# Four gate projections per GLA head, and the first neighbourhood projections beside the last head's rest

## The chip, the cores and the metric

The kernel runs on one core of a Trainium2 chip. Its engines are TensorE (PE), which multiplies matrices, VectorE (DVE), ScalarE (ACT), GpSimd (POOL) and SyncE (SP), whose queue issues the DMAs. Each engine works through its own list of instructions in order, and waits on semaphores for the others. The metric is the device time of one execution in microseconds (us), lower being better.

## The reference

The reference is a backbone of four layers for latent tokens: 1024 tokens of width 1024 on a grid 64 wide, with 256 context tokens ahead. Even layers mix by differential attention and a short gated convolution, odd layers by 2-D neighbourhood attention and a gated linear attention (GLA) that runs in both directions. The change touches the odd layer. Its mixer, cut to what matters:

```python
ck, cv, dk, dv, dlr, cq, dq, cg, dg = split_cols(h @ w_in, ODD_SIZES)
...
gf, gb = gla_log_gates(dlr, gate_up, gate_bias)
qh, kh, vh = to_bht(dq, GLA_DK) * qscale, to_bht(dk, GLA_DK), to_bht(dv, GLA_DV)
_, of = gla_scan(qh, kh, vh, gf, s_f)
_, ob = gla_scan(flip_t(qh), flip_t(kh), flip_t(vh), flip_t(gb), s_b)
o_gla = gla_out(of + flip_t(ob), gnorm)
o_na = neighbourhood_attention(heads(cq, NA_DIM), heads(ck, NA_DIM), heads(cv, NA_DIM), kc_na, vc_na, rpb)
u = jnp.concatenate([o_na.reshape(bsz, seq, BRANCH_W) * jax.nn.silu(cg), o_gla * jax.nn.silu(dg)], axis=-1)
```

In a chunk of the scan, with b the running sum of the log gates, the reference computes

```python
new = exp(b_end) * state + einsum('bhsd,bhse->bhde', kc * exp(b_end - b), vc)
o_inter = einsum('bhtd,bhde->bhte', qf * exp(b), state)
att = einsum('bhtd,bhsd,bhtsd->bhts', qf, kc, decay)     # decay[t, s] = exp(b[t] - b[s]) for s <= t
o = o_inter + einsum('bhts,bhse->bhte', att, vc)
```

There are 4 GLA heads (keys of 128, values of 256) and 16 neighbourhood heads of 64. cg and dg are the gate projections: sixteen blocks of 128 columns, whose SiLU multiplies the outputs.

## The kernel before, in words

**Projections.** Activations and weights are kept as a high and a low part, and a product is made of three (high by high, low by high, high by low). The activations' parts are hA and hB (two buffers, with an h or l behind). A weight unit is 1024x128: it comes by DMA as wraw, ACT casts it to whi (L242), POOL subtracts for wlo (L243). One step of a unit is 24 products `pj` (L438) over one chunk of tokens, 512 columns or 256. The object `ws` hands out steps in the order in which `units1` yields the units: `ws.run(n)` makes the next n, and between units stand named gates. `ws.open(name)` first finishes what stands ahead of a gate, then passes it.

**The GLA head.** `gla_head` walks two groups of 512 tokens (g = 1, 2), each in seven levels (lev 0 to 6; a level's blocks are L = 2^lev long), in `gla_levels`. At each level ACT makes exponentials KQ (L1151), DVE multiplies them by keys and queries (L1153) and adds to the running sums, which are called R in group 1 and g_u in group 2 (L1162), and PE makes the products gl (L1120). Their blocks are merged into att: below L = 32 by one predicated copy of DVE under a mask (L1132), else by copies of ACT, L rows high (L1136). After the levels `gla_exps` makes KH (exponentials on ACT, L1187 and L1188, product on DVE, L1189), g_qb (its product on POOL, L1193) and QF (L1198). `gla_chunk` takes a chunk of 128 tokens: transposes gktr of KH (L1213), split into gkh and gkl, products gu (L1233), the state Sn with its split Sh and Sl (L1258, L1261, L1262), outputs go (L1245). `gla_rest` follows: the last group's chunks, the backward outputs gob (L1337), norms, the transposes gotr (L1362), the multiplication by the stored gate (gsg, L1363), and the store into uT. It gives way twelve times, and a step is run each time.

**Gates.** A gate unit has two steps. Each ends with a tanh on ACT (L213), a product gt on DVE (L214) and a store to sgT (L983). Twelve of the sixteen gate units are run in the scans, three a head, one step at levels 0, 2 and 4 of each group; the last four stand in the rest of head 3.

**Neighbourhood attention.** `na` has 64 units (i, m, bp): eight pairs of heads i, the head m of the pair, a pair of query blocks bp. A unit makes query parts nqd, scores NS (L1464, L1465), bias and minimum on DVE (np, L1468), exp on ACT (L1470), scaling on POOL (L1472), transposes ntr (L1513) split into pth and ptl, and outputs nav (L1490). The bias nB comes from a mask namask and rows nG by DMA (POOL, L1423). Each pair i needs the projections ck (keys nk, L1378), cv (values, transposes nvtr) and cq: eight steps. `ws.until("cq0")` runs the first pair's ahead of everything, and one step goes with each unit after that.

**Order.** Tile's scheduler sets the order on each engine from priorities (the order of the code, moved by `high_priority`) and from when tiles are free. Tiles live in pools; a pool opened over the space of another waits for what was last done there. The neighbourhood pool stands where the GLA's pools stood, and its first tiles wait for the last stores of these.

Of the kernel before, what the change touches and what calls it, by code (L numbers as in the profile page):

```python
# [98 lines left out]
class Kernel:  # L99
# [20 lines left out]
    def setup(self):  # L120
# [20 lines left out]
        self.colsA = c.tile([P, 96], F32, name="colsA")  # L141
# [655 lines left out]
    def out0(self, conv_es, es):  # L797
# [13 lines left out]
        self.mod_finish(0, "g")  # L811
        self.mod_finish(1, "a")
# [126 lines left out]
    def units1(self):  # L939
# [47 lines left out]
    def layer1(self, post, out_es):  # L987
        nc, ws = self.nc, self.ws
        ws.open("gla")
        with ExitStack() as es:  # L990
# [22 lines left out]
        with ExitStack() as es:  # L1013
            ap = self.ap = self.pool("na", ctx=es)
            self.ps_s = self.pool("ps_s1", bufs=1, space=PSUM, ctx=es)
            self.gate_tile = lambda: ap.tile([P, 640], F32, name="gt", tag="np", bufs=5)[:, 0:512]
            self.na()


    def gla_setup(self):  # L1020
# [26 lines left out]
    def gla_v(self, e, ci, t0, tn, ps):  # L1047
# [4 lines left out]
        t = self.gp1.tile([P, 512], F32, name="gvt", tag="T", bufs=2)  # L1052
# [231 lines left out]
    def gla_head(self, h, rest):  # L1284
# [13 lines left out]
        for g in (1, 2):  # L1298
            for lev, _ in enumerate(self.gla_levels(g, R, outs[g])):
# [341 lines left out]
```

## Time and profile before

| | us |
|---|---|
| median of 3 runs | 3097.12 |
| lowest, highest | 3093.14, 3097.38 |
| the profiled execution | 3095.47 |
| its span in the trace | 3093.7 |
| PE busy in the span | 2942.9 (95%) |
| DVE busy | 1879.2 (61%) |
| ACT busy | 1530.6 (49%) |
| POOL busy | 965.5 (31%) |

The profile is of one execution. Busy is the time in which an engine has an instruction under way; PE's matmuls overlap, so that a busy PE is not PE at its peak. The granted clock of PE has a mean of 0.987 of full speed over the span. Layer 1 begins near 1640 us of the span; the heads of the GLA run to some 2285, the neighbourhood attention to 2930, and the last output projection to the end.

### The profile page before, as it was taken

The numbers are of one execution on the slowest core, as the hardware profiler recorded it, in microseconds if no ns is written. First come the engines' busy times: TensorE is split into PE (matmuls) and PEld (weight loads), VectorE is DVE, ScalarE is ACT, GpSimd is POOL, SyncE is SP. The second block draws the span as 40 slices with busy tenths as digits, with TensorE's granted clock in tenths as the row PEclk, the third lists the DMA queues.
The fourth block names the chain that finished last, engine by engine and source line by source line (L and its number), as shares of the span: only waits on it lengthen the run. The fifth ranks groups of instructions, "written<-read, shape, count | busy, mean of one in ns | idle before, by whom it ended". The sixth has DMA issues, their size and how long they took to land. (4 is left out here: it accounts for less than half of the span.)

```text
span 3093.7 us, 42416 instructions
## 1 busy us (share of the span) xinstructions
PE 2942.9 (95%) x16244; PEld 2452.9 (79%) x16244; DVE 1879.2 (61%) x3149; ACT 1530.6 (49%) x2853; POOL 965.5 (31%) x765
## 2 busy tenths in 40 slices
PE   6999999999999999999999998999999999999898
PEld 4888888888888887888877777778777888887686
DVE  5675757575665757564244767575736666667723
ACT  4553535353544445453344665665635555556522
POOL 3213130313021211205233232322235555556622
PEclk9999999999999999999999999999999999999999
DMA  6111111211110211115342112111131111112323
GB/s 227 35 45 48 49 46 33 65 35 58 35 58 28 65 35 48 45 42 207 111 149 74 45 35 72 50 48 58 55 95 31 47 49 44 43 44 98 118 75 123
DMA packets 236982, 206.46 MB, mean 67 GB/s; under 512 B 43591, under 2 KB 194538, under 8 KB 236778
## 3 DMA queue, kind: packets, MB, share of 16 engines
q1 hardware_dynamic: 236778, 203.74, 21.4%
q8 instruction: 128, 2.10, 0.3%
q14 instruction: 76, 0.62, 0.1%
HBM read 168.04 MB, written 35.67 MB: 66 GB/s over the span
## 5 line engine op out<-in xcount | busy, mean ns | idle before, releaser
L243 POOL TENSOR_TENSOR wlo<-wraw,whi 128x1024 fp32r<-128x1024 f32 x149 | 371.6, 2494 | 1164.5 <-ACT whi L242 1014.9
L438 PE MATMUL pj<-hBh,whi 128*128 128x512 f32 (+1 forms) x1712 | 382.0, 353 | 9.7 <-ACT hBh L354 4.8
L438 PE MATMUL pj<-hBl,whi 128*128 128x512 f32 (+1 forms) x1712 | 370.3, 350 | 0.9 <-DVE hBl L355 0.9
L438 PE MATMUL pj<-hBh,wlo 128*128 128x512 f32 (+1 forms) x1712 | 350.7, 345 | 0.0
L242 ACT CAST whi<-wraw 128x1024 fp32r<-128x1024 f32 x176 | 184.5, 1048 | 308.7 <-PE ops L754 188.3
L438 PEld LDWEIGHTS pj<-hBh,whi 128*128 128x128 f32 x1712 | 275.3, 191 | 45.2 <-ACT hBh L354 5.4
L438 PEld LDWEIGHTS pj<-hBh,wlo 128*128 128x128 f32 x1712 | 278.7, 191 | 37.2
L438 PEld LDWEIGHTS pj<-hBl,whi 128*128 128x128 f32 x1712 | 279.5, 193 | 35.7 <-DVE hBl L355 1.1
L438 PE MATMUL pj<-hAh,whi 128*128 128x512 f32 x968 | 279.5, 409 | 14.6 <-ACT ropex L517 13.0
L438 PE MATMUL pj<-hAh,wlo 128*128 128x512 f32 x968 | 255.3, 398 | 0.0
L438 PE MATMUL pj<-hAl,whi 128*128 128x512 f32 x968 | 254.6, 394 | 0.0
L592 DVE TENSOR_REDUCE st<-S 128x1 f32<-128x1280 f32 (+1 forms) x160 | 203.8, 1274 | 79.3 <-PE S L590 79.3
L594 ACT ACTIVATE p<-S,st 128x1280 f32<-128x1280 f32 (+1 forms) x160 | 186.1, 1163 | 82.1 <-DVE st L592 80.5
L1472 POOL TENSOR_TENSOR np<-np,nst 128x640 f32<-128x640 f32 x128 | 166.6, 1304 | 192.3 <-DVE nst L1471 154.4
L438 PEld LDWEIGHTS pj<-hAh,wlo 128*128 128x128 f32 x968 | 181.0, 189 | 36.1
L438 PEld LDWEIGHTS pj<-hAh,whi 128*128 128x128 f32 x968 | 170.2, 191 | 47.9 <-ACT ropex L517 14.4
L438 PEld LDWEIGHTS pj<-hAl,whi 128*128 128x128 f32 x968 | 178.1, 189 | 34.7
L590 PE MATMUL S<-kst,qd 128*128 128x512 f32 (+1 forms) x832 | 192.3, 361 | 0.2 <-ACT p L594 0.2
L590 PEld LDWEIGHTS S<-kst,qd 128*128 128x128 f32 x832 | 137.1, 188 | 40.2 <-ACT p L594 21.5
L1468 DVE CUSTOM_DVE_ANT_0 np<-NS,nB 128x640 f32<-128x640 f32 x128 | 105.3, 823 | 90.4 <-PE NS L1465 84.5
L615 ACT CAST ath<-atr 128x512 fp32r<-128x512 f32 (+1 forms) x208 | 99.2, 505 | 113.5 <-PE atr L612 112.9
L1523 DVE TENSOR_TENSOR ptl<-ntr,pth 128x512 fp32r<-128x512 f32 (+2 forms) x224 | 117.5, 536 | 49.6 <-ACT pth L1522 45.7
(361 smaller groups left out, 6219.3 us busy)
## 6 DMA issues: line engine op xcount, KB each, us to landing
wraw<-in_ev_w_in_dram SPq DMA_DIRECT2D x64, 512.0 KB, 4.1
wraw<-in_od_w_in_dram SPq DMA_DIRECT2D x56, 512.0 KB, 3.9
wraw<-in_w_out_dram SPq DMA_DIRECT2D x55, 512.0 KB, 3.8
wraw<-in_w_mod_dram SPq DMA_DIRECT2D x48, 512.0 KB, 3.8
sgT<-gt SPq DMA_DIRECT2D x32, 256.0 KB, 2.0
uT<-sg SPq DMA_DIRECT2D x8, 640.0 KB, 3.5
nG<-in_rpbp_dram SPq DMA_DIRECT2D x128, 40.0 KB, 2.3
xt<-in_x_dram SPq DMA_DIRECT2D x8, 512.0 KB, 5.9
```

Source lines behind the costliest of these rows:

```text
L242: nc.scalar.copy(out=hi, in_=u.raw)
L243: (nc.vector if u.lo_eng == "v" else nc.gpsimd).tensor_tensor(out=lo, in0=u.raw, in1=hi.bitcast(F32), op=ALU.subtract)
L438: nc.tensor.matmul(ps[:, 0:tn], lhsT=a[:, k, :], rhs=self.h_at(k, t0, tn)[b], start=n == 0, stop=n == 23)
L590: nc.tensor.matmul(S[:, c0:c0 + tn], lhsT=qd[:, 2 * m + part, P * qt:P * qt + P], rhs=self.kst[m][:, t0:t0 + tn], start=part == 0, stop=pa ...
L592: nc.vector.tensor_reduce(out=st[:, m:m + 1], in_=S[:, 0:n], axis=AX.X, op=ALU.max, negate=True)
L594: nc.scalar.activation(out=p[m][:, 0:n], in_=S[:, 0:n], func=AF.Exp, bias=st[:, m:m + 1], accum_out=st[:, 2 + m:3 + m])
L615: nc.scalar.copy(out=dh, in_=tv)
L1468: nc.vector.tensor_tensor_reduce(out=p, in0=S[:, z0:z0 + 640], in1=bias[2 * i + m][:, c0:c0 + 640], scale=1.0, scalar=3e38, op0=ALU.add, o ...
L1472: nc.gpsimd.tensor_tensor(out=p, in0=p, in1=st[:, 2:3].broadcast_to([P, 640]), op=ALU.mult)
L1523: nc.vector.tensor_tensor(out=lv[:, s:e], in0=tr[:, s:e], in1=hv[:, s:e].bitcast(F32), op=ALU.subtract)
```

## The change

The gate units are handed out 4, 4, 4 and 3 to the heads' scans, in another order, and a step is run at levels 0, 2, 4 and 6 of each group. One gate unit is left for head 3's rest. A gate "na1" lets the first neighbourhood projections follow it: in head 3's rest, after its four chunks, `early_na` closes the pools gla1 and gla3 (a new pool that holds Gst, R, att, dec, KH, ql, qh, gkh and gkl) and opens the pool na1 in their space, for nk, nkh, nq, nv, nvt and nvx. The gate "na" stands behind cq0 now, `ws.until("cq0")` is gone, and two steps follow the first scores, not one. The mask lmask has a sixth level, so L = 32 is merged by DVE too. The ring of two tiles T (gt, gvt, graw, QF, gsq, gsg) moves from gla1 to gla2, on the other side of the memory; lrx takes the tag KQ; colsA goes to the rope pool; nvx has its own tile; and the calls of mod_finish are gathered at the end of layer 0's attention. Hunks that only replace one pool by another are left out below.

```diff
--- before.py
+++ after.py
...
@@ -361,6 +360,7 @@
         self.new_h("A")
         self.new_h("B")
         cs = self.pool("rope", ctx=es0)
+        self.colsA = cs.tile([P, 96], F32, name="colsA")
         self.onesD = cs.tile([P, P], F32, name="onesD")
         nc.vector.memset(self.onesD, 1.0 / D)
         self.cos = cs.tile([P, SEQ], F32, name="cos")
@@ -506,6 +506,8 @@
             for h in range(8):
                 self.diff_head(h)
                 self.ws.open(f"head{h + 1}")
+        for l, what in ((0, "g"), (1, "a"), (1, "g")):
+            self.mod_finish(l, what)
         rope_es.close()
         return conv_es
 
...
@@ -952,8 +952,8 @@
             u.hold = u.extra = n == "dq0"
             yield u
         yield "gla0"
-        gates = [8, 9, 0, 1, 10, 11, 2, 12, 13, 3, 14, 15]
-        per = [3, 3, 3, 3]
+        gates = [8, 9, 0, 1, 10, 11, 2, 3, 12, 13, 4, 5, 14, 15, 6, 7]
+        per = [4, 4, 4, 3]
         for h in range(4):
             if h:
                 yield self.proj(f"dk{h}", self.w1(self.DK, h), CHUNKS, lambda *a: self.gla_k(*a))
@@ -964,15 +964,14 @@
             for k in gates[sum(per[:h]):sum(per[:h + 1])]:
                 yield self.gate_unit(k)
             yield f"end{h}"
-        yield self.gate_unit(4)
-        yield self.gate_unit(5)
-        yield self.gate_unit(6)
         yield self.gate_unit(7)
-        yield "na"
+        yield "na1"
         for i in range(8):
             yield self.proj(f"ck{i}", self.w1(self.CK, i), CHUNKS, lambda *a, i=i: self.na_k(i, *a))
             yield self.proj(f"cv{i}", self.w1(self.CV, i), CHUNKS, lambda *a, i=i: self.na_v(i, *a))
             yield self.proj(f"cq{i}", self.w1(self.CQ, i), CHUNKS[:2], lambda *a, i=i: self.na_q(i, *a))
+            if i == 0:
+                yield "na"
         yield "out1"
 
     def gate_unit(self, k):
@@ -987,9 +986,11 @@
     def layer1(self, post, out_es):
         nc, ws = self.nc, self.ws
         ws.open("gla")
+        self.N, n_es = {}, self.ctx.enter_context(ExitStack())
         with ExitStack() as es:
-            self.gp1 = self.pool("gla1", ctx=es)
-            self.gate_tile = lambda: self.gp1.tile([P, 512], F32, name="gt", tag="T", bufs=2)
+            g_es = es.enter_context(ExitStack())
+            self.gp1 = self.pool("gla1", ctx=g_es)
+            self.gate_tile = lambda: self.gp.tile([P, 512], F32, name="gt", tag="T", bufs=2)
             self.gla_setup()
             with ExitStack() as es2:
                 self.we = self.pool("we", ctx=es2, bufs=1)
@@ -999,11 +1000,18 @@
                 out_es.close()
                 for f in self.early.values():
                     f()
-            self.mod_finish(1, "g")
             self.gp = self.pool("gla2", ctx=es, side="right")
+            self.gp3 = self.pool("gla3", ctx=g_es)
             ws.prefetch()
             self.ps_l = self.pool("ps_l", bufs=2, space=PSUM, ctx=es)
             ws.open("gla0")
+
+            def early_na():
+                ws.open("na1")
+                g_es.close()
+                self.n1 = self.pool("na1", ctx=n_es)
+
+            self.early_na = early_na
             rest = self.gla_pre(0)
             for h in range(4):
                 rest = self.gla_head(h, rest)
@@ -1013,22 +1021,22 @@
         with ExitStack() as es:
             ap = self.ap = self.pool("na", ctx=es)
             self.ps_s = self.pool("ps_s1", bufs=1, space=PSUM, ctx=es)
-            self.gate_tile = lambda: ap.tile([P, 640], F32, name="gt", tag="np", bufs=5)[:, 0:512]
             self.na()
+        n_es.close()
 
 
     def gla_setup(self):
         nc, A = self.nc, self.A
         self.lrS = self.gp1.tile([P, TOK], F32R, name="lrS")
         nc.vector.memset(self.lrS.bitcast(F32), 0.0)
-        self.lmask = self.gp1.tile([P, 5, P], mybir.dt.uint8, name="lmask")
-        m = self.gp1.tile([P, 5 * P], mybir.dt.int32, name="lmask32", tag="gkq")
+        self.lmask = self.gp1.tile([P, 6, P], mybir.dt.uint8, name="lmask")
+        m = self.gp1.tile([P, 6 * P], mybir.dt.int32, name="lmask32", tag="gkq")
         nc.sync.dma_start(m, A["lmask"])
         nc.vector.tensor_copy(self.lmask.rearrange("p a b -> p (a b)"), m)
 
     def gla_lr(self, ci, t0, tn, ps):
         nc = self.nc
-        x = self.gp1.tile([32, 512], F32, name="lrx", tag="T", bufs=2)
+        x = self.gp1.tile([32, 512], F32, name="lrx", tag="KQ", bufs=2)
         nc.scalar.copy(out=x[:, 0:tn], in_=ps[0:32, :])
         hi = self.lrS[0:32, t0:t0 + tn]
         nc.scalar.copy(out=hi, in_=x[:, 0:tn])
...
@@ -1121,14 +1129,14 @@
             return ps.rearrange("p (c t) -> p c t", t=P)
 
         def own():
-            out["att"] = gp.tile([P, nch, P], F32, name="att", tag="att")
+            out["att"] = self.gp3.tile([P, nch, P], F32, name="att", tag="att")
             ps = product(kf[:, t0:t0 + n], qf[:, t0:t0 + n])
             nc.vector.scalar_tensor_tensor(out=out["att"], in0=ps, scalar=2.0,
                                            in1=self.ident.rearrange("p (o t) -> p o t", o=1).broadcast_to([P, nch, P]), op0=ALU.mult, op1=ALU.mult)
 
         def others(lev, k, q):
             ps, att, L = product(k, q), out["att"], 1 << lev
-            if L < 32:
+            if L < 64:
                 nc.vector.copy_predicated(att, self.lmask[:, lev:lev + 1, :].broadcast_to([P, nch, P]), ps)
             else:
                 for r in range(0, P, L):
...
@@ -1300,7 +1308,7 @@
                 if lev in (0, 1, 3, 4, 5):
                     nxt = self.gla_chunk(g - 1, todo.pop(0), outs[g - 1]) if todo else None
                     S, behind = behind(S) if behind else S, nxt
-                if lev in (0, 2, 4):
+                if lev % 2 == 0:
                     ws.run(1)
                 if g == 1 and lev == 4:
                     R2 = self.gla_gates(h, 2)
@@ -1320,6 +1328,8 @@
             S, behind = behind(S), nxt
             next(pre, None)
             yield
+        if h == 3:
+            self.early_na()
         S = None
         ms = gp.tile([P, 8], F32, name="gms", tag="gms")
         for c in (9, 8, 7, 6, 5, 4, 3, 2, 1, 0):
...
@@ -1537,11 +1546,10 @@
                 nc.gpsimd.tensor_tensor(out=u[:, 512 * c:512 * c + 512], in0=u[:, 512 * c:512 * c + 512], in1=s, op=ALU.mult)
                 nc.sync.dma_start(self.uT[1][i][:, 512 * c:512 * c + 512], u[:, 512 * c:512 * c + 512])
 
-        ws.until("cq0")
         bias[0] = self.na_bias(0)
         units = [(i, m, bp) for i in range(8) for m in range(2) for bp in range(4)]
         nxt = scores(*units[0])
-        ws.run(1)
+        ws.run(2)
         for n, (i, m, bp) in enumerate(units):
             ps_ = nxt
             if bp == 1 and 2 * i + m < 15:
...
```

How it moves instructions is shown at three places. The first is DVE in a GLA head, at the end of group 1: R's addition is the last of group 1 (level 6), g_u's addition of 128x2x512 the first of group 2. Before:

```order
L1162 TENSOR_TENSOR R<-R 128x8x2x64
L1153 TENSOR_TENSOR KQ<-KQ,gkq 128x1024
L1162 TENSOR_TENSOR g_u<-g_u 128x2x512
L1189 TENSOR_TENSOR KH<-KH,gkq 128x1024
L1198 TENSOR_TENSOR QF<-QF,gkq 128x512
L1156 TENSOR_TENSOR KQ<-KQ,gkq 128x512
L214 SCALAR_TENSOR_TENSOR gt<-gt,pj 128x512
```

After:

```order
L1170 TENSOR_TENSOR R<-R 128x8x2x64
L1161 TENSOR_TENSOR KQ<-KQ,gkq 128x1024
L213 SCALAR_TENSOR_TENSOR gt<-gt,pj 128x512
L1197 TENSOR_TENSOR KH<-KH,gkq 128x1024
L1206 TENSOR_TENSOR QF<-QF,gkq 128x512
L1170 TENSOR_TENSOR g_u<-g_u 128x2x512
L1164 TENSOR_TENSOR KQ<-KQ,gkq 128x512
```

The addition on g_u stands behind KH and QF instead of ahead of them, and a gate product stands ahead of KH. It is so in all four heads.

The second place is PE in the same stretch of head 2, from the products of level 6 on. Before:

```order
L1120 MATMUL gl<-KQ 128x128 x4
L1120 MATMUL gl<-gkq 128x128 x4
L438 MATMUL pj<-hAl,whi 128x512 x2
L1213 MATMUL gktr<-ident,KH 128x128 x3
L438 MATMUL pj<-hAl,whi 128x512 x2
L438 MATMUL pj<-hAh,wlo 128x512 x2
L1120 MATMUL gl<-KQ,gkq 128x128 x4
L438 MATMUL pj<-hAh,wlo 128x512
```

After:

```order
L1128 MATMUL gl<-KQ 128x128 x4
L1128 MATMUL gl<-gkq 128x128 x4
L438 MATMUL pj<-hAl,whi 128x512 x2
L1221 MATMUL gktr<-ident,KH 128x128
L438 MATMUL pj<-hAl,whi 128x512 x2
L438 MATMUL pj<-hAh,wlo 128x512 x8
L1221 MATMUL gktr<-ident,KH 128x128 x2
L1241 MATMUL gu<-gvh,gkh 128x256
L1128 MATMUL gl<-KQ,gkq 128x128 x4
```

The first gktr keeps its place; one transpose stands there instead of three, and the rest of the step's products come ahead of the next. A further whole step follows a few rows later.

The third place is PE where the neighbourhood attention begins, between the last transposes of the GLA's output and the second pair of scores. Before:

```order
L438 MATMUL pj<-hAh,whi 128x512 x8
L438 MATMUL pj<-hAl,whi 128x512 x2
L1464 MATMUL NS<-nk_19311,nqd 128x384
L1465 MATMUL NS<-nk_19311,nqd 128x256
L1464 MATMUL NS<-nk_19311,nqd 128x384
L1465 MATMUL NS<-nk_19311,nqd 128x256
L438 MATMUL pj<-hAl,whi 128x512 x5
L1464 MATMUL NS<-nk_19311,nqd 128x384
L1465 MATMUL NS<-nk_19311,nqd 128x256
```

After:

```order
L1372 MATMUL gotr<-ident,g_u 128x128 x8
L438 MATMUL pj<-hBh,whi 128x512 x8
L438 MATMUL pj<-hBl,whi 128x512 x8
L438 MATMUL pj<-hBh,wlo 128x512 x8
L438 MATMUL pj<-hAh,whi 128x512 x8
L438 MATMUL pj<-hAl,whi 128x512 x2
L1473 MATMUL NS<-nk_19101,nqd 128x384
L1474 MATMUL NS<-nk_19101,nqd 128x256
L1473 MATMUL NS<-nk_19101,nqd 128x384
L1474 MATMUL NS<-nk_19101,nqd 128x256
L438 MATMUL pj<-hAl,whi 128x512 x6
L438 MATMUL pj<-hAh,wlo 128x512 x8
```

The first scores stand 34 products behind the last gotr; before, all of ck0, cv0 and cq0 stood between the two. Behind the first four score products a longer run of projection products follows, where the next four came after five before.

## Rows read from the trace of the kernel before

**Rows 1.** The page's busy table: busy us, share of the span, instructions
```profile
PE 2942.9 (95%) x16244; PEld 2452.9 (79%) x16244; DVE 1879.2 (61%) x3149; ACT 1530.6 (49%) x2853; POOL 965.5 (31%) x765
```

**Rows 2.** Windows of layer 1: length, busy (count) of each engine, TensorE clock, DMA
```profile
core 0: us, PE busy (x) PEld busy (x) DVE busy (x) ACT busy (x) POOL busy (x), PEclk, DMA share, GB/s
...
2002.00:2145.00 143.00, 131.36 (x736) 110.61 (x735) 99.12 (x140) 87.08 (x194) 41.80 (x32) 0.98 0.18 54
2145.00:2285.00 140.00, 127.16 (x670) 104.84 (x668) 86.40 (x123) 69.89 (x162) 36.80 (x30) 0.98 0.25 78
2285.00:2330.00 45.00, 38.65 (x191) 32.58 (x191) 13.79 (x24) 12.55 (x21) 16.75 (x18) 0.96 0.29 69
2330.00:2840.00 510.00, 494.22 (x2929) 422.08 (x2930) 344.36 (x734) 283.40 (x606) 283.50 (x305) 1.00 0.17 44
2840.00:2930.00 90.00, 76.39 (x425) 61.90 (x424) 70.71 (x128) 56.66 (x114) 59.00 (x49) 0.96 0.37 122
```

**Rows 3.** Waits of PE, 1722:2285: total us, times, longest us
```profile
PE gktr L1213 <- DVE KH L1189: 13.4, 8, 2.9
PE gl L1120 <- DVE KQ L1153: 8.2, 8, 1.8
...
PE go L1245 <- DVE Sl L1262: 6.3, 4, 1.7
...
PE gotr L1362 <- ACT g_u L1353: 1.7, 1, 1.7
```

**Rows 4.** Timeline of PE, head 2: start, length, operation, [idle before <-releaser]
```profile
2040.58 1.13 PE L1120 MATMUL gl<-KQ 128*128 128x128 f32 x8 [1.13 <-DVE KQ L1153]
...
2046.00 0.63 PE L1213 MATMUL gktr<-ident,KH 128*128 128x128 f32 x3 [2.93 <-DVE KH L1189]
...
2066.73 0.39 PE L1245 MATMUL go<-Sl,qh 128*128 128x256 f32 x1 [1.52 <-DVE Sl L1262]
```

**Rows 5.** Timeline of DVE, the same stretch of head 2
```profile
2038.07 1.23 DVE L1162 TENSOR_TENSOR R<-R 128x1024 f32<-128x1024 f32 x1 [1.12 <-ACT KQ L1151]
2039.21 1.22 DVE L1153 TENSOR_TENSOR KQ<-KQ,gkq 128x1024 f32<-128x1024 f32 x1
2040.43 3.31 DVE L1162 TENSOR_TENSOR g_u<-g_u 128x1024 f32<-128x1024 f32 x1
2043.66 2.28 DVE L1189 TENSOR_TENSOR KH<-KH,gkq 128x1024 f32<-128x1024 f32 x1
...
2064.07 2.60 DVE L1262 TENSOR_TENSOR Sl<-Sn,Sh 128x256 fp32r<-128x256 f32 x1
```

**Rows 6.** Timeline of POOL, the same stretch
```profile
2039.75 2.91 POOL L243 TENSOR_TENSOR wlo<-wraw,whi 128x1024 fp32r<-128x1024 f32 x1 [1.78 <-ACT whi L242]
2042.62 2.25 POOL L1193 TENSOR_TENSOR g_qb<-g_qb,gkq 128x512 f32<-128x512 f32 x1
...
2063.07 3.33 POOL L243 TENSOR_TENSOR wlo<-wraw,whi 128x1024 fp32r<-128x1024 f32 x1 [6.74 <-ACT KQ L1151]
```

**Rows 7.** Timeline of ACT, the same stretch
```profile
2038.06 0.53 ACT L1136 COPY att<-gl 32x128 f32<-32x128 f32 x2
...
2040.95 0.62 ACT L1188 ACTIVATE KH<-R 128x512 f32<-128x512 f32 x1
```

**Rows 8.** Windows, the five us behind the wait of head 2
```profile
2045.00:2050.00 5.00, 4.00 (x16) 3.61 (x17) 2.95 (x5) 2.62 (x7) 2.15 (x3) 0.66 0.31 103
```

**Rows 9.** Lines by form, 1722:2285: count, busy us, mean ns, idle before
```profile
L1262 DVE TENSOR_TENSOR Sl<-Sn,Sh 128x256 fp32r<-128x256 f32 x72 | 45.6, 634 | 18.3 <-ACT Sh L1261 17.6
...
L1132 DVE COPY_PREDICATED att<-lmask,gl 128x512 f32<-128x512 uint8 x40 | 29.5, 739 | 9.6 <-PE gl L1120 9.5
```

**Rows 10.** Waits of PE, 2285:2345, where the neighbourhood attention begins
```profile
PE pj L438 <- DVE nk L1378: 3.8, 1, 3.8
```

**Rows 11.** Timeline of PE, 2296:2300, an undisturbed projection step
```profile
2296.37 1.98 PE L438 MATMUL pj<-hAh,wlo 128*128 128x512 f32 x8
2298.19 1.98 PE L438 MATMUL pj<-hBh,whi 128*128 128x512 f32 x8
```

More of the change, by code (lines that the diff above doesn't have):

```diff
@@ L139, in setup @@
         nc.vector.tensor_reduce(out=self.sel, in_=self.ident.rearrange("p (j x) -> p x j", x=32)[:, 0:2, :], axis=AX.X, op=ALU.add)
-        self.colsA = c.tile([P, 96], F32, name="colsA")
         self.colsB = c.tile([P, 35], F32, name="colsB")
@@ L810, in out0 @@
             self.load_u(0, k, 4, 6, *ring(768))
-        self.mod_finish(0, "g")
-        self.mod_finish(1, "a")
         self.gg = [up.tile([P, D], F32, name=f"gg{s}") for s in range(2)]
@@ L1051, in gla_v @@
             self.gvl = self.gp1.tile([P, 10, 256], F32R, name="gvl", tag="gvl")
[L1052 removed]
+        t = self.gp.tile([P, 512], F32, name="gvt", tag="T", bufs=2)
         nc.scalar.copy(out=t[:, 0:tn], in_=ps)
@@ L1066, in gla_gate_w @@
         nc, A, gp = self.nc, self.A, self.gp
-        raw = self.gp1.tile([P, 512], F32, name="graw", tag="T", bufs=2)[0:32, 0:256].rearrange("p (a b) -> p a b", a=2)
+        raw = self.gp.tile([P, 512], F32, name="graw", tag="T", bufs=2)[0:32, 0:256].rearrange("p (a b) -> p a b", a=2)
         nc.vector.memset(raw, 0.0)
@@ L1070, in gla_gate_w @@
         nc.sync.dma_start(raw[16:32, 1, :], A["od_gate_up"][0, 1][:, P * h:P * h + P])
-        self.Gst = gp.tile([P, 2, P], F32R, name="Gst", tag="Gst")
+        self.Gst = self.gp3.tile([P, 2, P], F32R, name="Gst", tag="Gst")
         nc.vector.memset(self.Gst[96:128].bitcast(F32), 0.0)
@@ L1088, in gla_gates @@
         else:
-            R = gp.tile([P, 2048], F32, name="R", tag="R")
+            R = self.gp3.tile([P, 2048], F32, name="R", tag="R")
         X, Y = R[:, 0:2 * n], R[:, 1024:1024 + 2 * n]
@@ L1182, in gla_exps @@
         kf, qf, pl = self.kf, self.gqf, self.plane
-        dec = out["dec"] = gp.tile([P, 4], F32, name="dec", tag="dec", bufs=2)
+        dec = out["dec"] = self.gp3.tile([P, 4], F32, name="dec", tag="dec", bufs=2)
         nc.scalar.activation(out=dec[:, 0:nch], in_=pl(R, 1024 + P - 1, [P, nch]), func=AF.Exp, scale=1.0 / 16)
         nc.scalar.activation(out=out["db"][:, c0:c0 + nch], in_=pl(R, 1024 + n, [-P, nch], at=n - 1), func=AF.Exp, scale=1.0 / 16)
-        KH = out["KH"] = gp.tile([P, 2, 512], F32, name="KH", tag="KH")[:, :, 0:n]
+        KH = out["KH"] = self.gp3.tile([P, 2, 512], F32, name="KH", tag="KH")[:, :, 0:n]
         nc.scalar.activation(out=KH[:, 0, :], in_=R[:, 0:n], func=AF.Exp, scale=1.0 / 16)
@@ L1193, in gla_exps @@
             nc.gpsimd.tensor_tensor(out=qb, in0=qb, in1=qf[:, tk], op=ALU.mult)
-            ql = out["ql"] = gp.tile([P, 512], F32R, name="ql", tag="ql")
-            qh = out["qh"] = gp.tile([P, 512], F32R, name="qh", tag="qh")
-            q = self.gp1.tile([P, 512], F32, name="QF", tag="T", bufs=2)
+            ql = out["ql"] = self.gp3.tile([P, 512], F32R, name="ql", tag="ql")
+            qh = out["qh"] = self.gp3.tile([P, 512], F32R, name="qh", tag="qh")
+            q = self.gp.tile([P, 512], F32, name="QF", tag="T", bufs=2)
             nc.scalar.activation(out=q, in_=R[:, 1024:1536], func=AF.Exp, scale=1.0 / 16)
@@ L1214, in gla_chunk @@
         a, b = P * dirs[0], P * dirs[-1] + P
-        kh = gp.tile([P, 256], F32R, name="gkh", tag="gkh", bufs=2)
-        kl = gp.tile([P, 256], F32R, name="gkl", tag="gkl", bufs=2)
+        kh = self.gp3.tile([P, 256], F32R, name="gkh", tag="gkh", bufs=2)
+        kl = self.gp3.tile([P, 256], F32R, name="gkl", tag="gkl", bufs=2)
         nc.scalar.copy(out=kh[:, a:b], in_=tr[:, a:b])
@@ L1368, in na_k @@
     def na_k(self, i, ci, t0, tn, ps):
-        nc, ap = self.nc, self.ap
+        nc = self.nc
         if ci == 0:
-            self.N[i] = dict(k=[ap.tile([P, TOK], F32R, name=f"nk{m}", tag=f"nk{m}", bufs=2) for m in range(2)])
+            self.N[i] = dict(k=[self.n1.tile([P, TOK], F32R, name=f"nk{m}", tag=f"nk{m}", bufs=2) for m in range(2)])
         kst = self.N[i]["k"]
-        hi = ap.tile([P, 512], F32, name="nkh", tag="nkh")[:, 0:tn]
+        hi = self.n1.tile([P, 512], F32, name="nkh", tag="nkh")[:, 0:tn]
         nc.scalar.copy(out=hi.bitcast(F32R), in_=ps)
@@ L1381, in na_q @@
         if ci == 0:
-            self.N[i]["q"] = self.ap.tile([P, SEQ], F32, name="nq", tag=f"nq{i % 2}")
+            self.N[i]["q"] = self.n1.tile([P, SEQ], F32, name="nq", tag=f"nq{i % 2}")
         self.nc.scalar.mul(out=self.N[i]["q"][:, t0:t0 + tn], in_=ps, mul=-0.125)
     def na_v(self, i, ci, t0, tn, ps):
-        nc, ap = self.nc, self.ap
+        nc = self.nc
         if ci == 0:
-            self.N[i]["v"] = ap.tile([P, 10, 2, 2, 64], F32R, name="nv", tag="nv", bufs=2)
-            self.N[i]["vt"] = ap.tile([P, SEQ], F32, name="nvt", tag=f"nq{i % 2}")
+            self.N[i]["v"] = self.n1.tile([P, 10, 2, 2, 64], F32R, name="nv", tag="nv", bufs=2)
+            self.N[i]["vt"] = self.n1.tile([P, SEQ], F32, name="nvt", tag=f"nq{i % 2}")
         vst, vt = self.N[i]["v"], self.N[i]["vt"]
@@ L1395, in na_v @@
         else:
-            vt = ap.tile([P, 640], F32, name="nvx", tag="np", bufs=5)
+            vt = self.n1.tile([P, 256], F32, name="nvx", tag="nvx")
             nc.scalar.mul(out=vt[:, 0:tn], in_=ps, mul=0.5)
@@ L1578, in level_masks @@
     x = s ^ t
-    return np.concatenate([(x >> lev == 1).astype(np.int32) for lev in range(5)], axis=1)
+    return np.concatenate([(x >> lev == 1).astype(np.int32) for lev in range(6)], axis=1)
 def window_masks():
```

5 lines of the change are left out of this document (2 added, 3 removed).

## The prediction

> **What bounds the kernel now.** I read the page's busy table first, then windows of layer 1, then TensorE's (PE) waits, then the timelines of the other engines around the two longest waits. The table shows PE busy for 2942.9 us, 95% of the span [rows 1]; no other engine comes near. So the kernel is bound by PE, and an edit can only win time in which PE stands still or runs at a low clock, or lose by adding such time. No product is removed here.
>
> The windows say where PE stands still [rows 2]. The neighbourhood attention's steady part has only 510.00 − 494.22 = 15.8 us of idle PE in 510. The heads of the GLA have 143.00 − 131.36 = 11.6 us (head 2) and 140.00 − 127.16 = 12.8 us (head 3) each, though DVE, busy for 99 and 86 us there, and ACT, for 87 and 70, are far from full. The 45 us between GLA and neighbourhood attention have 6.4 us, at a clock of 0.96, and the 90 us of the last neighbourhood units 13.6 us.
>
> The waits of the four heads [rows 3] put names to this: the transpose gktr waits 13.4 us for KH, the level products gl 8.2 us for KQ, the output go 6.3 us for Sl. In head 2 the timeline [rows 4] has 1.13 us ahead of gl at 2040.58 and 2.93 us ahead of gktr at 2046.00, 4.06 in all, at level 6 of group 1; heads 0, 1 and 3 repeat it, four of the eight waits in the 13.4 us being the long ones. The five microseconds behind that wait have a granted clock of 0.66 [rows 8], between the two levels of 1.2 and 2.4 GHz, after PE had nearly nothing to do: 4.00 us busy at 0.66 instead of 1 is 4.00 x 0.34 = 1.4 us. Together 5.4 us a head.
>
> Why is KH late? DVE [rows 5] does R's addition at 2038.07, KQ at 2039.21, and then the addition on g_u, which already belongs to the next group: 3.31 us, where the same shape takes 1.23 at 2038.07. It ends at 2043.74; POOL's weight split wlo ran from 2039.75 to 2042.66 [rows 6]. KH then takes 2.28 us, not 1.22 like KQ, while POOL's g_qb runs from 2042.62 for 2.25. ACT had KH's exponentials ready at 2041.57 [rows 7], so DVE's order and POOL's holds made the wait.
>
> A page of the Trainium skill, SBUF — State Buffer, section "SBUF: two separate sides", states that VectorE and GpSimd share one port pair as an exclusive lock: an operation of VectorE with two SBUF inputs and a GpSimd operation that reads SBUF exclude each other for a whole instruction, whoever starts first. The trace agrees (3.31 against 1.23 us), and by that rule the time hangs on who starts first in the new order, which is rival 1.
>
> **The change part by part.** (a) *Level 6.* The new DVE order puts g_u's addition behind KH and QF, and a gate product (gt) ahead of KH. The six-level mask also takes two pairs of 32-row copies out of ACT's queue ahead of KQ's exponentials, one pair of which takes 0.53 us [rows 7]; so KQ's inputs come about 1 us sooner. That brings KQ's start to about 2038.7, and the weight split, which follows the cast one place ahead of it on ACT, moves sooner as well, to about 2038.7: a dead heat. If KQ starts first, KH follows after 1.22 + some 0.7 (the gate product) and I estimate PE waits of about 0.5 + 1.3 = 1.8 us; if the split starts first, KQ is held until about 2041.1 and the waits are some 2.9, not 4.06. The middle is 2.4; with the shorter wait I let the clock loss go: 5.4 − 2.4 = 3.0 a head, **12 us** for four. The bounds are 4 x 1.1 = 4 (split first, clock loss stays) and 4 x 5 = 20 (waits nearly filled).
>
> The added projection step itself does not cover this wait: in PE's new order the first gktr still stands two products behind the level-6 products, and the added step comes after it.
>
> (b) *The stretch behind it.* Between the first gktr and the transposes of group 2's first chunk PE now has 82 projection products instead of 65 in heads 0 to 2, and 76 in head 3. Eight products of 512 columns take 2298.19 − 2296.37 = 1.82 us [rows 11], so 17 are 3.9 us of filler. It can fill the waits for KQ, gkl and Sl that the listed totals leave: beyond level 6, head 2 has 11.6 − 4.1 = 7.5 us idle. Against it stands what DVE gains: one predicated merge a group, 0.74 us each [rows 9], 1.5 a head, the moved addition of 1.2 us, and one more weight split on POOL, which can hold a DVE operation for 3.31 − 1.23 = 2.1 us. ACT loses eight copies a head, some 2 us, and gains a tanh pair. PE's filler of 3.9 is set against a DVE that has 143 − 99 = 44 us free in the head, but not in this stretch. I take 1.7 us in each of heads 0 to 2 and 1 in head 3: **6 us**. The bounds are 14 (all filler counts) and −4 (the moved addition counts on the path in all heads).
>
> (c) *End of head 3.* The wait of gotr for g_u, 1.7 us [rows 3], and of pj for nk, 3.8 us [rows 10], come from the neighbourhood pool opening only when the last gated rows are stored. With ck0, cv0 and cq0 beside the rest, neither need be there, and the low clock of 45 us at 0.96 [rows 2], 1.8 us, should go. That is 7.3; the new nk tiles must in turn wait for the pools of the scan to be free, so I take **6 us**, with bounds 0 and 7.3. The mask and bias chain of the first scores is still behind the last store, but PE's new order has 108 products of 512 columns between the last gotr and the first probability transpose, 108 / 8 x 1.82 = 24.6 us [rows 11], beside 24 narrower ones, and I let them hide it.
>
> (d) *Neighbourhood attention.* Its start has the projections bunched: PE's order has 98 projection products ahead of the second unit, then 6, 4 and 5, where it had 24 before each. Its end has one more unit with none. The last stretch, whose units have hardly any projection, idles 13.6 us in 90 [rows 2], with some eight units of the 64, 1.7 each, against 15.8 us over some 53 units, 0.3, in the steady part. So four bare units cost 4 x 1.4 = 5.6, and I take **−6 us**, with bounds 0 (probability work runs ahead under the bunched products) and −10.
>
> (e) *Tile moves.* The T ring, colsA and the mod_finish calls move: the layer-0 order on PE stays as it was. Gst now stands over weights of dq0 and graw's transfer waits for a store; I count −0.5 us, once, between 0 and −2.
>
> Sum: 12 + 6 + 6 − 6 − 0.5 = 17.5 us less. The profiled execution is 3095.47 us, its span 3093.7; 3095.47 − 17.5 = 3078.0. The median of the runs is 1.65 above the profiled one: **3079.6**, said as 3079.5.
>
> **Rivals.** *1, the weight split wins everywhere.* POOL starts wlo before KQ in each scan and holds it; the clock loss stays, so (a) gives the difference of the waits alone, (4.06 − 2.9) x 4 = 4.6, (b) half, 3. For it speaks how close the starts are, against it that ACT also has a gate's tanh to do ahead. 4.6 + 3 + 6 − 6 − 0.5 = 7.1: 3090. By the Trainium skill's rule on the shared port pair (SBUF — State Buffer, the section named above) an early split does just this, and the row of g_u's addition bears it out.
>
> *2, slower: the state chain.* In group 2 the new PE order has go and gu of the four chunks with only two to four projection products between them, so Sn, Sh and Sl follow one another in the open. Sl takes 0.63 us on average [rows 9] and 2.60 at 2064.07 under the split that began at 2063.07 [rows 5, 6], for a wait of 1.52 [rows 4]. If three of four chunks in each head lose 2.2 us, that is 12 x 2.2 = 26 against 17.5: 3079.5 + 26 = 3105.5. It decides from eight chunks on, 17.5 / 2.2. Against it: one split per step cannot fall on three chunks, and PE's units gu and go of other chunks lie between.
>
> *3, the filler is only exchanged.* The steps that fill the scans are missing at the seam, where (c) turns into new waits of nk for the scan's tiles (0), and (d) is at its bound of −10, (b) 0: 12 − 10 − 0.5 = 1.5, 3095.6. This is also the time if the change does little of what it says.
>
> *4, better.* KQ first in all heads and (b) twice my value, with (d) at −3: 16 + 12 + 6 − 3 − 0.5 = 30.5, 3066.6.
>
> **How the numbers follow.** Forecast 3079.5 with 0.50; rival 1 with 0.16; rival 3 with 0.12; rival 2 with 0.07; rival 4 with 0.15. A measurement of this kernel can tell about 0.2%, 6 us, from no change. Faster means below 3090.9: forecast, rival 4 and most of rival 1, 0.77. Within 0.2%, 3090.9 to 3103.3: rival 3 and the rest of rival 1, 0.16. Slower: 0.07. The range goes from 3064, a little below rival 4, to 3094, above rival 1; outside lie rival 2 and most of rival 3, under 0.2.
>
> **What would show it.** (a) the wait of the first gktr for KH at level 6 below 1.5 us in most heads, KH 1.2 us long, and the clock of the next five microseconds near 1; rival 1 shows as KQ of over 3 us. (b) each head's window 1 to 3 us shorter beyond that. (c) no wait of pj for nk, and gotr without one. (d) more idle time in the first five neighbourhood units and the tail than the 16 and 14 us before. The prediction is wrong if KH stays over 2 us in all heads, or if go's waits for Sl pass 6.3 us by more than 10, or if the first scores wait for the bias.

## The result: slower, by half a percent

The changed kernel takes 3111.47 us (median of 4 runs, 3108.1 to 3113.73) against 3095.63 of the kernel before beside it (3093.14 to 3097.38). The ratio is 1.0051, with a 95% interval of 1.0033 to 1.0068. The forecast of 3079.5 was wrong, in its sign too. The profiled execution took 3112.84 us with a span of 3111.1, that is 17.4 more than the 3093.7 of before.

The busy table shows no new bound; PE is busy for the same share of a longer span (compare [rows 1]).

```profile
PE 2948.6 (95%) x16244; PEld 2463.5 (79%) x16244; DVE 1890.8 (61%) x3157; ACT 1523.8 (49%) x2821; POOL 972.7 (31%) x765
```

The windows of layer 1 answer to [rows 2]: heads 2 and 3 of the GLA, the seam, the neighbourhood attention and its end (columns as there).

```profile
2013.00:2162.00 149.00, 140.59 (x768) 119.70 (x767) 98.36 (x142) 87.60 (x188) 41.12 (x32) 0.97 0.19 56
2162.00:2296.00 134.00, 124.58 (x702) 105.36 (x701) 88.41 (x131) 68.78 (x158) 40.15 (x35) 0.97 0.22 68
2296.00:2336.00 40.00, 36.51 (x181) 30.14 (x180) 17.39 (x38) 14.38 (x27) 17.89 (x21) 0.96 0.29 77
2336.00:2856.00 520.00, 472.45 (x2762) 403.12 (x2762) 349.21 (x702) 270.93 (x581) 276.26 (x290) 0.98 0.16 41
2856.00:2947.00 91.00, 79.00 (x446) 64.56 (x445) 73.84 (x139) 59.85 (x124) 62.90 (x53) 0.96 0.35 118
```

The heads lost idle time, as forecast: head 2 now idles 149.00 − 140.59 = 8.4 us, against 11.6. But the neighbourhood attention, which idled 15.8 us in 510, idles 520.00 − 472.45 = 47.6 us in 520. Most of its units have as many projection products beside them as before.

Where the time went is plainest from the scores NS. These two rows, of the kernel before and the changed kernel, give the count of the wider score products, their lengths, and when the first and the last of them began.

```profile
L1464 PE MATMUL NS<-nk,nqd x256: 338/362/660, 2322.9 to 2909.5; 128*128 128x384 f32 x128
```
```profile
L1473 PE MATMUL NS<-nk,nqd x256: 342/362/657, 2303.1 to 2928.7; 128*128 128x384 f32 x128
```

The first score came 2322.9 − 2303.1 = 19.8 us sooner: up to there the change gained most of what it was forecast to gain. From first to last score it took 625.6 us instead of 586.6, 39.0 more. What follows was 1.8 us shorter: 39.0 − 19.8 − 1.8 = 17.4. So the question is what made 64 neighbourhood units slower by 39 us.

The order answers half of it. The units have a cycle of eight (one pair of heads), and so have the projection steps: ck with 512, 512 and 256 columns, cv the same, cq with 512 and 512. One step goes with one unit, so which step lies beside which unit is fixed by how many steps ran ahead of the loop. The kernel before ran the first pair's eight and one more; the changed kernel runs the eight and two more, because `ws.run(1)` behind the first scores became `ws.run(2)`. From there on every unit has its neighbour's step. The narrow step of ck, which lay in unit 18 of the kernel before (and 26, 34, ...), now lies in unit 17.

These windows show units 17 and 18 (from first score to first score) before the change, and units 25 and 26, their like, after it, in a cycle whose granted clock stayed at 1.00. Each pair of units holds the same work: one wide step and one narrow.

```profile
2480.87:2490.32 9.45, 9.45 (x54) 7.87 (x52) 6.48 (x14) 4.91 (x10) 5.45 (x6) 1.00 0.17 56
2490.32:2497.59 7.27, 6.94 (x53) 6.51 (x52) 5.86 (x14) 5.35 (x12) 4.46 (x8) 1.00 0.20 74
```
```profile
2559.93:2565.74 5.81, 5.71 (x45) 5.50 (x44) 4.86 (x10) 4.38 (x8) 2.45 (x3) 1.00 0.06 20
2565.74:2580.60 14.86, 10.74 (x63) 8.98 (x61) 10.79 (x19) 5.90 (x15) 9.98 (x11) 1.00 0.31 99
```

16.72 us became 20.67, of which PE idles 4.2 instead of 0.3. That is 3.95 of the some 5.5 us by which eight units grew: the window of eight is 75.79 us before and 81.27 after, with the same 73.5 us of busy PE.

```profile
2474.11:2549.90 75.79, 73.46 (x434) 62.58 (x435) 51.33 (x110) 42.16 (x90) 42.07 (x45) 1.00 0.18 44
```
```profile
2550.31:2631.58 81.27, 73.47 (x435) 62.79 (x434) 54.67 (x109) 42.13 (x90) 42.72 (x45) 1.00 0.16 41
```

The changed kernel has six such pairs of units. In four of them, units 17 and 18 among these, the granted clock fell too, and the pair takes 21.5 to 21.9 us.

Now the other half, why the narrow step hurts there. The timelines of PE, DVE and POOL in units 17 and 18 of the changed kernel, one fence for each engine, and last the same cast of DVE in e1_run1, the kernel of the first experiment below:

```profile
2482.58 1.12 PE L438 MATMUL pj<-hBh,wlo 128*128 128x256 f32 x8
2483.54 0.36 PE L1473 MATMUL NS<-nk,nqd 128*128 128x384 f32 x1
...
2487.33 0.53 PE L1499 MATMUL nav<-ptl,nv 128*128 128x256 f32 x1 [1.79 <-DVE ptl L1532]
...
2495.97 0.47 PE L1499 MATMUL nav<-pth,nv 128*128 128x256 f32 x2 [1.49 <-DVE nu L1505]
```
```profile
2484.20 2.43 DVE L1462 CAST nqd<-nqd 64x512 fp32r<-64x512 f32 x1
2486.85 0.42 DVE L1532 TENSOR_TENSOR ptl<-ntr,pth 128x256 fp32r<-128x256 f32 x1
```
```profile
2483.90 2.45 POOL L242 TENSOR_TENSOR wlo<-wraw,whi 128x1024 fp32r<-128x1024 f32 x1 [0.35 <-ACT whi L241]
```
```profile
2471.35 0.42 DVE L1462 CAST nqd<-nqd 64x512 fp32r<-64x512 f32 x1
```

The narrow step is over at 2483.5, the next scores come at once, and PE's order has little else ahead of the outputs nav, whose probabilities still go through DVE. Just there POOL begins the next weight split at 2483.90. DVE's cast of nqd, 0.42 us in e1_run1, takes 2.43 until the split ends, ptl starts behind it, and PE waits 1.79 us; a second wait of 1.49 follows, for nu. In units 25 and 26 the two waits are 1.84 and 1.78 us. In the kernel before a wide step of some 5.5 us lies over this place, and its waits in units 17 and 18 name no ptl.

### The profile page after: what moved, and what is told of

The parts are those of the page before. It is cut to its first block, busy times and chain, and to the rows that moved or that the text cites. A ratio compares the mean times of both kernels' runs of the same rounds, so it can differ in the third digit from the quotient of the medians.

```text
span 3111.1 us, 42394 instructions
## 1 busy us (share of the span) xinstructions
PE 2948.6 (95%) x16244; PEld 2463.5 (79%) x16244; DVE 1890.8 (61%) x3157; ACT 1523.8 (49%) x2821; POOL 972.7 (31%) x765
## 5 line engine op out<-in xcount | busy, mean ns | idle before, releaser
L592 PEld LDWEIGHTS S<-kst,qd 128*128 128x128 f32 x832 | 137.0, 188 | 40.3 <-ACT p L596 21.5
L1531 ACT CAST pth<-ntr 128x512 fp32r<-128x512 f32 (+2 forms) x224 | 101.2, 461 | 84.2 <-PE ntr L1522 46.4
```

The lines of the kernel that those rows point to most:

```text
L592: nc.tensor.matmul(S[:, c0:c0 + tn], lhsT=qd[:, 2 * m + part, P * qt:P * qt + P], rhs=self.kst[m][:, t0:t0 + tn], start=part == 0, stop=pa ...
L1531: nc.scalar.copy(out=hv[:, s:e], in_=tr[:, s:e])
```

## Experiments

Each was compared with the kernel before on its own chip, whose median was 3096.09 us beside the first four, 3095.42 beside e1_ck021 and p_run3, and 3096.31 beside the others. Times are medians; the ratio is made from all runs and can differ a little from that of the medians.

| run | what | us | ratio to before, 95% interval |
|---|---|---|---|
| e1_run1 | changed, one step behind the first scores | 3074.34 | 0.9937 (0.9924 to 0.9949) |
| b_run2 | before, two steps there | 3127.32 | 1.0106 (1.0090 to 1.0121) |
| b_scan | before, gates and levels of the change | 3090.42 | 0.9985 (0.9977 to 0.9994) |
| a_noscan | e1_run1 with the gates and levels of before | 3088.13 | 0.9975 (0.9965 to 0.9985) |
| m_ck021 | changed, narrow step of ck one earlier | 3088.67 | 0.9977 (0.9967 to 0.9987) |
| e1_ck021 | e1_run1, narrow step of ck one earlier | 3085.83 | 0.9969 (0.9958 to 0.9979) |
| p_run3 | changed, three steps behind the first scores | 3089.98 | 0.9981 (0.9972 to 0.9990) |
| a_lm5 | e1_run1, level 5 merged by ACT | 3079.23 | 0.9945 (0.9933 to 0.9957) |
| v_0245 | e1_run1, steps at levels 0, 2, 4, 5 | 3085.55 | 0.9966 (0.9954 to 0.9979) |
| v_1356 | e1_run1, steps at levels 1, 3, 5, 6 | 3082.80 | 0.9957 (0.9943 to 0.9971) |

**The shift alone, taken out of the changed kernel and put into the one before.**

```diff
         nxt = scores(*units[0])
-        ws.run(2)
+        ws.run(1)
```

> The changed kernel with one step instead of two behind the first scores; nothing else. Theory 1 (phase): the second step put the projection steps one unit ahead of the neighbourhood units, so that a narrow step (256 columns) falls on another unit of each group of eight; then the eight units take 75.9 us again instead of 81.3, the stretch from the first to the last score 587 to 592 us instead of 625.8, and the time is 3073 to 3080 us. Theory 2 (the early start or the new pools for nk, nv and nvx slow the units, whatever the phase): the eight units stay at 80 to 82 us and the time at 3106 to 3112 us.

> The kernel before with two steps instead of one behind the first scores; nothing else. Theory 1 (phase): eight units take 81.3 us instead of 75.9, seven times, so 3096 + 38 = 3133 us (3126 to 3138). Theory 2 (early start or pools): 3092 to 3100 us, the units as before.

Both came out as theory 1 has it. Without the second step the changed kernel takes 3074.34 us and is faster than both; with it the kernel before is slower by 31 us. The scores of the two, as in the rows of the result:

```profile
L1473 PE MATMUL NS<-nk,nqd x256: 342/362/660, 2302.0 to 2894.1; 128*128 128x384 f32 x128
```
```profile
L1464 PE MATMUL NS<-nk,nqd x256: 342/363/522, 2320.7 to 2940.9; 128*128 128x384 f32 x128
```

592.1 us with the right step beside each unit, in the changed kernel, and 620.2 with the wrong one, in the kernel before, against 586.6. The early start, the pools and the bunched steps have no part in the 33 us that separate 625.6 from 592.1; they make at most the 5.5 that are left. In the kernel before the shift costs 620.2 − 586.6 = 33.6 us, in the changed one 625.6 − 592.1 = 33.5: the same, whatever else is changed. The 38 expected for b_run2 were seven cycles of eight units at 5.4 each. Only the second to the sixth cycle lost as much, 5.5 to 6.5 us each and 29.7 together; the first, the seventh and the rest make 4.0 together.

**What of the shift costs: the narrow step, or the weight splits?**

```diff
-            yield self.proj(f"ck{i}", self.w1(self.CK, i), CHUNKS, lambda ...
+            yield self.proj(f"ck{i}", self.w1(self.CK, i), [CHUNKS[0], CHUNKS[2], CHUNKS[1]], lambda ...
```

> The changed kernel, two steps behind the first scores as it stands, with the three steps of the key projection ck in the order 512, 256, 512 columns instead of 512, 512, 256. The weight splits and all steps of cv and cq keep their units; only the narrow step moves, from the third unit of each eight (18, 26, ...) to the one ahead. Theory M1 (the phase costs because the narrow step is too short a cover for the unit it falls on): the idle 5 to 6 us of units 18, 26, ... go, the eight units take 75 to 78 us, the time is 3074 to 3088 us. Theory M2 (it costs because of where the weight splits fall): the eight units stay at 80 to 82 us, the time at 3106 to 3113 us.

> The changed kernel with one step behind the first scores (3074 us), and the key projection's steps in the order 512, 256, 512. This puts the narrow step of ck on the same unit of each eight on which the changed kernel has it, while the weight splits and all other steps stay as in the 3074 us kernel. M1 (the narrow step's place makes most of the loss): eight units take some 79 us instead of 75.9 (the 3.3 us that moving it took away in the reverse direction), PE's idle time in the third unit rises to about 5 us, and the time is 3092 to 3101 us. M2 (the weight splits' places make it): 3071 to 3080 us.

(A unit is named there by the scores that the step's products stand ahead of; above it is named by the scores behind which they come, one less.) In the changed kernel this edit alone brings back 22.8 of the 37 us, 3111.47 to 3088.67; that is 0.7 above the range of M1 and far below that of M2. The other way round, in e1_run1, it costs 11.5, between the two expectations. The windows of eight units, m_ck021 and e1_ck021:

```profile
2463.22:2540.97 77.75, 73.42 (x436) 62.73 (x434) 52.07 (x109) 42.37 (x90) 42.73 (x45) 1.00 0.16 43
```
```profile
2454.83:2532.23 77.40, 73.50 (x434) 62.47 (x435) 51.57 (x110) 42.45 (x90) 42.13 (x45) 1.00 0.17 43
```

So neither theory was whole. The narrow step in unit 17 alone adds 77.40 − 75.84 = 1.6 us to eight units (75.84 is e1_run1's window). The shift with the narrow step moved off unit 17, into unit 16, adds 77.75 − 75.84 = 1.9. The shift as it is adds 81.27 − 75.84 = 5.4, 1.9 more than the two. The trace of e1_ck021 shows why: PE's waits there are those of the short cover alone, and the weight split lies a unit later. The windows are its units 17 and 18; PE's waits and the split follow.

```profile
2461.59:2467.36 5.77, 5.77 (x45) 5.46 (x44) 4.85 (x10) 4.25 (x8) 3.19 (x4) 1.00 0.04 11
2467.36:2480.37 13.01, 10.57 (x63) 8.83 (x61) 8.19 (x19) 6.35 (x15) 7.76 (x10) 1.00 0.21 77
```
```profile
2470.08 0.55 PE L1522 MATMUL ntr<-ident,np 128*128 128x128 f32 x3 [0.87 <-POOL np L1481]
2476.61 0.48 PE L1499 MATMUL nav<-pth,nv 128*128 128x256 f32 x2 [1.57 <-DVE nu L1505]
```
```profile
2480.68 2.40 POOL L242 TENSOR_TENSOR wlo<-wraw,whi 128x1024 fp32r<-128x1024 f32 x1 [3.51 <-PE pj L438]
```

The wait for nu is there, 1.57 us, as in the changed kernel; the wait of 1.79 for ptl is not, for the split begins at 2480.68, at the end of the stretch, and holds no cast of nqd. The two units take 5.77 + 13.01 = 18.78 us: of the 3.95, the short cover alone makes 18.78 − 16.72 = 2.06, and 1.89 come with the split. The split without the short cover stands in m_ck021: there it begins in unit 18 too, at 2481.17, but the cast of nqd was done at 2476.70, in 0.42 us. So it takes the short cover and the split in the same place to lose 3.95 us in those two units.

**A shift by one more step.**

```diff
-        ws.run(2)
+        ws.run(3)
```

> The changed kernel with three steps behind the first scores: the cycle shifted by one more step. The narrow step of ck then falls where the run with the moved narrow step had it. M1: the eight units take 77 to 79 us, one more unit at the end has no projection (2 us), and the time is 3085 to 3097 us, less than with two steps. If the loss grows with each step of shift, whatever the step's width: eight units of 84 us or more, over 3125 us.

3089.98: less than with two steps, and in the range of M1. The loss does not grow with the shift; it goes by what lands on what.

**The two halves of the change.** b_scan has only the list of gates and the levels; a_noscan has the rest.

```diff
-                if lev in (0, 2, 4):
+                if lev % 2 == 0:
```

> The kernel before with the gates 4, 4, 4 and 3 per head and a step at levels 0, 2, 4 and 6; the one gate left stands in head 3's rest; pools, mask and the start of the neighbourhood attention as before. If the added step makes the scans' gain, the last transposes of head 2 come some 21 us later for 32.7 us of added products (11.3 us gained, as in the changed kernel), and the time is 3083 to 3089 us, less what head 3's rest loses for want of steps (up to 6 us). If the shorter ACT list of the new mask made the gain, 3093 to 3098 us.

> The changed kernel with the gates 3 a head at levels 0, 2 and 4 as before, four gates in head 3's rest, and one step behind the first scores: the mask, the pools and the early neighbourhood projections alone. If the early projections make the seam's part of the gain (19.8 us at the first scores less 11.3 of the scans), 3085 to 3090 us; if the seam only exchanges waits, 3094 to 3098 us. With Theory 2 on the neighbourhood units it would be over 3115 us.

The scan's step alone gains 5.7 us, the rest alone 8.0, both 21.8. Each lies in the first of its two expectations, b_scan by the up to 6 us that it left for head 3's rest. They need each other. In b_scan, PE's waits of the stretch from 1722 to 2290 have two that the kernel before has smaller [rows 3, 10]:

```profile
PE pj L438 <- DVE nk L1375: 8.6, 1, 8.6
...
PE gotr L1359 <- ACT g_u L1350: 3.8, 1, 3.8
```

The gates that went into the scans are missing in head 3's rest, and 8.6 + 3.8 us of waits stand where 3.8 + 1.7 stood, 6.9 more, which is most of the 8.1 by which both together gain more than the sum. In the changed kernel the early neighbourhood projections fill that place: neither wait is there, and one of 2.5 us for nvx is what is new.

**Level 6 of the scan: whose hold, and is it worth taking away?** In the changed kernel the split won the race for KQ, in all four heads. The timelines of PE, DVE and POOL in head 2 answer to [rows 4, 5, 6], the window behind it to [rows 8]:

```profile
2056.68 1.44 PE L1128 MATMUL gl<-KQ 128*128 128x128 f32 x8 [2.92 <-DVE KQ L1161]
```
```profile
2053.14 3.40 DVE L1161 TENSOR_TENSOR KQ<-KQ,gkq 128x1024 f32<-128x1024 f32 x1
```
```profile
2052.98 2.47 POOL L242 TENSOR_TENSOR wlo<-wraw,whi 128x1024 fp32r<-128x1024 f32 x1 [0.69 <-ACT whi L241]
```
```profile
2055.00:2060.00 5.00, 3.32 (x17) 3.31 (x18) 4.16 (x4) 1.96 (x6) 2.66 (x2) 0.73 0.51 157
```

The split began 0.16 us ahead of KQ, KQ took 3.40 us instead of 1.22, and the wait of 2.93 for KH became one of 2.92 for KQ. Three kernels try to take this away: a_lm5 makes both later, v_0245 and v_1356 move the step whose weights are split there.

```diff
-            if L < 64:
+            if L < 32:
```
```diff
-                if lev % 2 == 0:
+                if lev in (0, 2, 4, 5):
```

> The changed kernel with one step behind the first scores (3074 us) and with the merge of level 5 by ACT's copies again, as before the change. The two copies ahead of level 6's exponentials bring KQ and the weight split about 1 us later each. If the new mask decides who starts first, KQ at level 6 takes 1.2 us instead of 3.4, PE's waits for KQ in the scans fall from 15.3 us to about 8, and the time is 3062 to 3070 us. If the scans are set elsewhere and the wait only moves, 3071 to 3080 us.

> The changed kernel with one step behind the first scores (3074 us) and the scan's steps at levels 0, 2, 4 and 5 instead of 0, 2, 4 and 6. In ACT's order the weight cast comes behind KH's and QF's exponentials, so POOL's split can't hold KQ at level 6. If that hold is what is left of the wait: KQ 1.2 us, the waits for KQ down by 4 x 1.8 us or more, the low clock behind them gone (4 x 1 us): 3060 to 3068 us. If a wait for KH or for the added step's place comes instead: 3070 to 3080 us.

> As the run before, with the scan's steps at levels 1, 3, 5 and 6; ACT's order has the weight cast behind the exponentials of KH and g_qb, and no step at level 0. If KQ's hold is what matters, 3060 to 3068 us as there; if the lack of a step at level 0 opens a wait at the group's start, 3070 to 3085 us.

PE's waits in the scans of a_lm5, then of v_0245:

```profile
PE gl L1128 <- DVE KQ L1161: 8.3, 8, 1.8
...
PE gl L1128 <- DVE KQ L1164: 3.9, 5, 1.5
PE gu L1241 <- DVE gkl L1226: 3.7, 3, 1.2
PE gl L1128 <- DVE att L1134: 3.0, 4, 0.8
```
```profile
PE gl L1128 <- DVE KQ L1164: 17.1, 5, 4.0
...
PE gl L1128 <- DVE KQ L1161: 5.4, 4, 2.2
```

In a_lm5 the waits for KQ fell to 8.3 us as the first theory wanted, but the three others, 1.8, 1.6 and 0.9 in the changed kernel, are 3.9, 3.7 and 3.0, and the time falls in the second range. Its median is 4.9 us above that of e1_run1, but the runs of the two overlap (3077.44 to 3080.37 and 3073.32 to 3079.16), so that it is slower is not shown; that it is not faster is. In v_0245 the same wait sits a level later, 4.0 us long, and the time, 3085.55, is above both expectations. DVE's timeline of head 2 shows what it stands behind: QF, 0.69 us long in the changed kernel, now takes 2.87 beside the split, which begins at 2061.15 there, and the addition on g_u and the awaited KQ come after it.

```profile
2061.88 2.87 DVE L1206 TENSOR_TENSOR QF<-QF,gkq 128x512 f32<-128x512 f32 x1
```

v_1356 falls in its second range; PE's largest wait in its scans is that of the outputs go for ACT's copies g_u, 8.1 us, and whether it comes of the step missing at level 0 was not examined. Taking the hold off KQ made no kernel faster: other waits came instead.

## Why the prediction was wrong

The step that failed is (d), the neighbourhood attention. It counted bare units, at the start and at the end, and took −6 with a bound of −10; the stretch from first to last score lost 39.0. The bare units were the smaller part of it: e1_run1 has the same bunched start, one bare unit fewer at the end, and 592.1 − 586.6 = 5.5 us, of which 4.9 lie in the first eight units (80.28 us against 75.36, with the same products). So the term as it was argued was right in size. What was left out is that `ws.run(2)` shifts all later units against their steps; that is the other 33.5 us. The prediction's own reading, 24 projection products before each unit, counted products and not their columns; 24 products of 256 columns and 24 of 512 look alike in such a count.

No rival named it either. Rival 2 put a slower outcome into the scans' state chain, and the waits of go for Sl, 6.3 us before [rows 3], are not among the seven longest of after; it fell. Rival 3, filler exchanged, fell too: the first score came 19.8 us sooner. The range, 3064 to 3094, did not reach the result because its lower bound for (d) was taken from units without steps, never from units with another step.

The other terms, by the marks of PE's trace:

- (a) was forecast as 12 with 4 for the case that the split comes first. It came first: 2.92 us instead of 4.06, and the low clock stayed in heads 1 to 3 (in head 2 0.73 against 0.66 [rows 8]); in head 0 the clock did not fall (1.00 from 1757 to 1762). So (a) is rival 1's 4.6 and, at the prediction's own price, 1.4 for head 0's clock: half of the 12. The dead heat was read rightly, though not its outcome.
- (b) came out near its size. The last transposes gotr of head 2 begin at 2160.83 instead of 2139.47, 21.4 us later, with six more steps in front. A step is 24 / 8 x 1.82 = 5.45 us [rows 11], six are 32.7, so 11.3 us were gained up to there; (a) and (b) together were to give 9 + 5 = 14 in three heads. Of the 11.3, 1.5 were there before the first head ((e) below) and (a) is 3 x 1.14 + 1.4 = 4.8, so that some 5.0 are left for (b), by subtraction alone. The waits of go for Sl that it was to fill, 6.3 us, are gone.
- (c), with head 3's share of (a) and (b), was to give 6 + 4 = 10. From those transposes to the first score it is 142.30 us instead of 183.41, with 32.7 us of steps fewer: 8.4.
- (e) was to cost 0.5; the first level product came 1.5 us sooner, and that is in the 11.3.

Up to the first score the forecast was 12 + 6 + 6 − 0.5 = 23.5 and the gain 19.8. In e1_run1 the first score comes 2322.9 − 2302.0 = 20.9 us sooner, the units take 5.5 more and what follows 2.8 less: its span of 3075.5 is 18.2 shorter than that of before, where the sum said 17.5 (by the medians it gains 21.8). So the sum held, for the kernel without the second step, and in part by luck: (a) gave half of its 12 us, and (d) with the end of the kernel cost 2.7 instead of 6. Of the signs that the prediction named, rival 1's KQ of over 3 us is there; gktr's wait for KH, pj's for nk and gotr's for g_u are gone; and the idle time of the neighbourhood units gave (d) away, though not where the sign was to be looked for: it lies in the steady part, while the tail idles 91.00 − 79.00 = 12.0 us, less than before.

Of the shift's loss outside units 17 and 18 of each eight, 1.5 us, the larger part lies in unit 19 or its like, where e1_run1 idles 0.8 us and the changed kernel 1.6, all of it one wait for ptl:

```profile
2588.12 0.39 PE L1499 MATMUL nav<-ptl,nv 128*128 128x256 f32 x1 [1.58 <-DVE ptl L1532]
```

m_ck021 has this wait too, 1.60 us long. What delays ptl there was not tried.

## What to carry to other kernels

Where filler steps of unequal length run beside a loop of unequal units, their phase is a parameter like any other: changing a step count ahead of the loop shifts every pairing after it, and the cost is multiplied by the number of cycles. Compare the new and old order not by the count of filler instructions beside each unit but by their time and kind, in the steady part too, even if the change is elsewhere. And a wait that ends on a shared resource may only move when its victim is put elsewhere; three ways to free KQ here gave no faster kernel.

## What was not expected of the hardware

The hold between POOL's split and DVE was expected for products of two tensors. It shows as well on a cast, with one input: nqd's 64x512 took 2.43 us under the split that began 0.30 us before it, and did so once in each of six cycles; the same cast took 0.42 in e1_run1. The Trainium skill, SBUF — State Buffer, section "SBUF: two separate sides", names as held, besides operations of VectorE with two SBUF inputs, those in a two-port performance mode; the trace agrees that this cast was held, and does not show its mode. The granted clock fell behind such stops in the neighbourhood attention too, between its levels of 2.4 and 1.2 GHz, but not each time: in the five microseconds in which unit 18 waits, PE is busy for 2.86 us at 0.74, while the window of unit 26 above, with waits as long, stays at 1.00.

```profile
2485.00:2490.00 5.00, 2.86 (x12) 2.27 (x12) 4.07 (x8) 0.98 (x4) 4.45 (x4) 0.74 0.40 109
```
